# A two-layer trunk in split float32: value products without ScalarE's copy, the last group's scores of layer a later, and halves of a wide output block between the first blocks' ends

## The chip, the core and the metric

One core of a Trainium2 chip runs the whole program. TensorE (PE) multiplies and transposes, and loads its stationary operand ahead (PEld); VectorE (DVE) and ScalarE (ACT) do all element-wise work; SyncE (SP) issues the transfers, which 16 DMA engines carry. Each engine runs its instructions strictly in the order in which they were put on it, and waits at each for what that one needs. The metric is the device time of one execution, in microseconds (us).

## The reference

Two pre-norm residual layers on a 256 x 2048 float32 input, 16 heads of 128. Layer a is latent attention, layer b attends within blocks of 256 positions; as the sequence is 256 long, layer b is causal attention with a linear distance penalty (the distance table times a slope for each head). Cut to what matters:

```python
def mla_mixer(h, ...):                       # layer a
    proj = h @ w_in                          # query latent 512, kv latent 256, rotary key 64, gate 2048
    q  = (rms_norm(q_lat) @ w_q_up)          # 16 heads x (128 + 64 rotary)
    kv = (rms_norm(kv_lat) @ w_kv_up)        # 16 heads x (128 key + 128 value)
    ...                                      # norms of q and k, rotary part
    o = causal_block_attention(q, k, v, scale)   # softmax(q k^T) v for each head
    return from_heads(o) * silu(gate)
x = x + mla_mixer(rms_norm(x, norm_a), ...) @ w_out_a
x = x + moba_mixer(rms_norm(x, norm_b), ...) @ w_out_b
```

## The kernel before

**Split products.** Weights are float32. A tile of 1024 columns (512 KB) comes by DMA into `wr` (4 buffers); ACT makes its high part `wh` (line 147, 1.05 us), DVE the rest `wl` (line 151, 1.2 us), both in the fast float32r form, and a product is three float32r matmuls (high x high, high x low, low x high). So every weight tile passes SP's queue, ACT's queue and DVE's queue before PE can use it. `run` keeps four tiles loaded ahead. A `wr` buffer is free again when the `wl` of the tile four places earlier is done, and the next load, which stands in SP's queue, waits for that; whatever stands behind that load on SP waits as well.

**A head** (`head_steps`) has steps that the planner places apart:
- s1: scores on PE (`ps_s`), the mask added and the minimum taken on DVE (line 468), exponentials on ACT (470), their reciprocal and the scaling of the weights `sm` on DVE (475).
- s2: `sm` is turned by a DMA transpose that SP issues (446): first a copy into `pz` as two planes (layer a: on ACT, line 445; layer b: on DVE), then the transpose, then a copy back into `pz` on DVE (452).
- s2_parts: from `pz` ACT makes `ph` (494) and, for the 128 columns of the first query half, the float32 copy `p1` (497); DVE makes `pl` (495).
- s3: four value products (`ps_o`), then `og` (value times gate) on DVE (509), and `ohl`, the high part on ACT (510) and the low part on DVE (511). `ohl` is what the output projection reads.

**Layer a** treats its 16 heads in 8 groups of two. `turns` of a group (three steps with transposes `ps_ta`, a copy and the parts `sr` of query and key, lines 425 to 431) come ahead of its scores.

**The output of layer a** has eight blocks of 256 columns, o0 to o7. A block takes 16 steps, one for each head; step i needs the `ohl` of head i, and four steps share one weight tile. Blocks o0 to o3 run their steps 0 to 11 first, since heads 12 to 15 (groups 6 and 7) are late, then their steps 12 to 15; then o4 to o7, which are of the wide kind (`blk_both`: each step writes two accumulators of a bank each). I write o1.4 for step 4 of block o1.

**Reloads.** Behind the last group, SP loads x again into `xt` (line 806, four loads) and then the distance table over the causal mask in `c_sb` (line 802, 192 KB). The first reader of that table is `alibi` of layer b's first head on ACT (line 917), which belongs to that head's s1.

**The order** of all steps on PE is written by a planner, `ordered(main, side)`: `main` is a fixed list; `side` steps (turns, heads) are put in when the lags of what they need have run out. Lags are constants: `TU` is that from a group's turns to its scores. What ACT, DVE and SP get follows from the order in which the steps are written out and from a scheduler.

Of the kernel before, what the change touches and what calls it, by code (L numbers as in the profile page):

```python
# [20 lines left out]
F32 = mybir.dt.float32  # L21
# [7 lines left out]
P = 128  # L29
S = 256  # L30
# [15 lines left out]

PA, PB, LO, TU, TUB, S1, S2A, S2B, S3 = 9000, 6000, 6000, 3000, 10000, 4800, 6000, 9000, 3000
FLB = 4500
SLACK = 1.3
HOLD = 4500  # L50
PACE, PACEB = 600, 3500
# [26 lines left out]
def paired(v):  # L78

    return v.rearrange("p (g l e) -> p g e l", l=2, e=16)  # L80


def lines(v):

    return v.rearrange("p (g l e) -> p g l e", l=2, e=16)


def unpaired(v):

    return v.rearrange("p (g e l) -> p g l e", l=2, e=16)  # L90
# [3 lines left out]
def trunk(ctx: ExitStack, tc, xT, gains, cst, w_in_a, w_q_up, w_kv_up, w_out_a, w_in_b, w_out_b, outT):  # L94
    nc = tc.nc
# [3 lines left out]
    wk = pool("wk", bufs=2)  # L99
# [55 lines left out]
    class Step:  # L155
# [7 lines left out]
        def ready(self):  # L163
            if any(d.end is None for d in self.needs + self.after):
                return None
            return max([d.end + d.lag * SLACK for d in self.needs], default=0)

# [30 lines left out]
    def matmul(*args, **kw):  # L198
        chain(nc.tensor.matmul(*args, skip_group_check=True, **kw))  # L199
# [254 lines left out]
    def head_steps(h, scores, bias, vt, cost, needs, needs_v, after, lag, front, pace=PACE, away=0):  # L454

        st = {}

        def s1():  # L460
            ps = work("ps_s")
            scores(ps)
            b = bias()
            sm = wk.tile([P, 384], F32, tag="sm", name="sm", bufs=3)
            mn = wk.tile([P, 2], F32, tag="mn", name="mn", bufs=4)
            rs = wk.tile([P, 2], F32, tag="rs", name="rs", bufs=4)
            for t, sl in ((0, slice(0, 128)), (1, slice(128, 384))):
                nc.vector.tensor_tensor_reduce(sm[:, sl], ps[:, sl], b[:, sl], 1.0, 3.0e38, ALU.add, ALU.min,  # L468
                                               mn[:, t:t + 1])
                nc.scalar.activation(sm[:, sl], sm[:, sl], AF.Exp, bias=mn[:, t:t + 1], scale=-1.0,  # L470
                                     accum_out=rs[:, t:t + 1])
            ri = wk.tile([P, 2], F32, tag="ri", name="ri", bufs=4)
            nc.vector.reciprocal(ri, rs)
            for t, sl in ((0, slice(0, 128)), (1, slice(128, 384))):
                nc.vector.tensor_scalar(sm[:, sl], sm[:, sl], ri[:, t:t + 1], None, op0=ALU.mult)
            st["p"] = sm

        def s2():
            pz = st["z"] = wk.tile([P, 384], F32, tag="pz", name="pz", bufs=2)
            if away:  # L480
                fly(st["p"], pz, front)
            else:
                flip(st["p"], pz, front)
                s2_parts()

        def s2_back():
            tc.keep_in_program_order(nc.vector.tensor_copy(words(st["z"]), planes(st["p"])))  # L487
            s2_parts()

        def s2_parts():  # L490
            pz = st["z"]
            ph = wk.tile([P, S], F32R, tag="ph", name="ph", bufs=2)
            pl = wk.tile([P, S], F32R, tag="pl", name="pl", bufs=2)
            nc.scalar.copy(ph, pz[:, :S])  # L494
            nc.vector.tensor_tensor(pl, pz[:, :S], ph.bitcast(F32), op=ALU.subtract)
            p1 = wk.tile([P, P], F32, tag="p1", name="p1", bufs=2)
            nc.scalar.copy(p1, pz[:, S:])
            st["t"] = ph, pl, p1

        def s3():  # L500
            po = work("ps_o")
            ph, pl, p1 = st["t"]
            vh, vl, v1 = vt()
            matmul(po[:, :S], vh, paired(ph), start=True, stop=False)
            matmul(po[:, :S], vh, paired(pl), start=False, stop=False)
            matmul(po[:, :S], vl, paired(ph), start=False, stop=False)
            matmul(unpaired(po[:, P:S]), v1, lines(p1), start=False, stop=True)
            og = wk.tile([P, S], F32, tag="og", name="og")
            nc.vector.scalar_tensor_tensor(og, po[:, :S], 0.5, gate_of[h // 2][:, h % 2], op0=ALU.mult, op1=ALU.mult)  # L509
            nc.scalar.activation(lines(ogh[:, h]), unpaired(og), AF.Copy)  # L510
            nc.vector.tensor_tensor(lines(ogl[:, h]), unpaired(og), lines(ogh[:, h].bitcast(F32)), op=ALU.subtract)  # L511

        a = Step(s1, cost, S1, needs, bank=True, pace=pace)
        b = Step(s2, 0, away or lag, [a])
        if away:
            e = Step(s2_back, 0, lag - away, [b])
            side.append(e)
        else:
            e = b
        return a, b, Step(s3, 545, S3, [e] + needs_v, after, bank=True, pace=pace)  # L520

    main, side = [], []
# [165 lines left out]
    heads, turns_of = [], []  # L688


    def group_a(g):
        z = {}
# [41 lines left out]
        def turn(i):  # L734
            def f():
                if i == 0:
                    two, four = (2, P), (2, S)
                    qf, kf, rf = cut(shared(g % 2), two, two, (1, P))
                    qh, ql, kh, kl, rh, rl = cut(shared(g % 2, F32R), two, two, four, four, (1, P), (1, P))
                    z["q"], z["k"], z["r"] = (qf, qh, ql), (kf, kh, kl), (rf, rh, rl)  # L740
                ps = work("ps_ta")
                if i == 2:
                    for t in range(2):
                        transpose(ps[:, t * P:(t + 1) * P], z["rope"][:, t].rearrange("p h d -> p (h d)"), ident)
                    parts(ps[:, :S], 1.0, *z["r"], False)
                    return
                for h in range(2):
                    for t in range(2):
                        transpose(ps[:, h * S + t * P:h * S + (t + 1) * P],
                                            z["tok", t][:, 256 * i + P * h:256 * i + P * (h + 1)], ident)  # L750
                if i == 0:
                    parts(ps, gq_a, *z["q"], False)
                else:
                    parts(ps, col(G_KN), *z["k"], True)
            return f

        def scores(h):
            def f(ps):
# [4 lines left out]

        proj = blk_rows(w_q_up[:, 384 * g:384 * (g + 1)], lambda: lat_st["x"], q_done)
        proj += blk_rows(w_kv_up[:, 512 * g:512 * (g + 1)], lambda: [x[:, 4:] for x in lat_st["x"]], kv_done, PA)
        turns = [Step(turn(i), 440, TU, proj[-1:], sum((h[:1] for h in heads[2 * g - 4:2 * g - 2]), ()) if g > 1 else (), bank=True)
                 for i in range(3)]
        for h in range(2):
            heads.append(head_steps(2 * g + h, scores(h), lambda: c_sb[:, C_MASK:C_MASK + 384],
# [57 lines left out]
    outs_a = [(blk_cols if j < 4 else blk_both)(w_out_a[:, 256 * j:256 * (j + 1)], og, out_done_a(j), 4000) for j in range(8)]  # L827
# [20 lines left out]
            outs_a[2 * j][-1].needs.append(again)  # L848
    for b in outs_a[:4]:
        main += b[:12]  # L850
    for b in outs_a[:4]:
        main += b[12:]
    main += sum(outs_a[4:], [])


    x_b = x_a
# [184 lines left out]
```

## Time and profile before

| | |
|---|---|
| time, median of 3 executions | 750.37 us (749.97 to 752.09) |
| the profiled execution's own time | 748.94 us |
| its span, first to last instruction | 747.1 us |
| PE busy | 739.7 us (99%) |
| PEld, DVE, ACT busy | 689.6 (92%), 588.3 (79%), 490.2 us (66%) |
| granted TensorE clock | 1.0 in every slice |
| DMA | 153.13 MB, mean 205 GB/s |

A share of busy time is a mean over the whole program. A PE that is 99% busy can gain only what is left of the span; it can lose anywhere. Start and end of a PE instruction overlap its neighbours', so the time lost on PE is read from the distance between starts.

### The profile page before, as it was taken

Reading aid. Unit: us, or ns where it says so; the run is one execution under the profiler, and the core shown is the slowest. Engines: PE = TensorE matmul, PEld = TensorE weight load, DVE = VectorE, ACT = ScalarE, POOL = GpSimd, SP = SyncE. Lnnn points to the kernel's source line nnn. Section 1 sums busy time; section 2 is a strip of 40 time slices with the busy share of each in tenths; the row PEclk is TensorE's granted clock in tenths of the full one; section 3 lists DMA queues with packets and bytes.
Section 4 is the critical chain, followed back from the end, with each engine's and each line's share of the span. In section 5 each row is a group of like instructions: output and inputs, shape, how many; then the busy total and the mean of one; then the engine's idle time right before and its main releaser. Section 6 shows DMA issues by size and latency. Waiting matters only on the chain.

```text
span 747.1 us, 13205 instructions
## 1 busy us (share of the span) xinstructions
PE 739.7 (99%) x4766; PEld 689.6 (92%) x4766; DVE 588.3 (79%) x1247; ACT 490.2 (66%) x1043; POOL 0.2 (0%) x4
## 2 busy tenths in 40 slices
PE   9999999999999999999999999999999999999998
PEld 8999999999999999988889888898889988899997
DVE  6988899899998697765788877887778967878563
ACT  7867898888877565456667666675567766665441
POOL 0000000000000000000000000000000000000000
PEclk9999999999999999999999999999999999999999
DMA  8875765666657866666888768886778778767771
GB/s 293 277 208 156 198 172 166 183 157 177 167 179 204 278 218 200 203 198 204 226 226 206 209 184 234 237 207 194 212 223 224 197 212 226 225 202 204 239 223 51
DMA packets 148354, 153.13 MB, mean 205 GB/s; under 512 B 47296, under 2 KB 115520, under 8 KB 148288
## 3 DMA queue, kind: packets, MB, share of 16 engines
q1 hardware_dynamic: 148000, 152.14, 71.7%
q8 instruction: 37, 0.61, 0.3%
q14 instruction: 29, 0.24, 0.1%
q10 hardware_dynamic: 288, 0.15, 0.1%
HBM read 139.68 MB, written 2.10 MB: 190 GB/s over the span
## 4 chain that ended last, share of the span: by engine, by line
PE 92%; DVE 3%; DMA 3%; ACT 0%; issue 0%; SPq 0%; DVEq 0%; ACTq 0%
PE acc L199 85%; PE ps_s L199 4%; DVE wl L151 2%; PE ps_o L199 2%; DMA sm<-pz 1%; PE ps_ta L202 1%; DMA c_sb<-cst 1%; DMA wr<-w_in_a 1%; ACT wh L147 0%; DVE xt L410 0%; PE ps_lt L202 0%; DVE xhl L334 0%; DVE pz L487 0%; PE ps_r L199 0%; DVE og L509 0%
## 5 line engine op out<-in xcount | busy, mean ns | idle before, releaser
L147 ACT ACTIVATE wh<-wr 128x1024 fp32r<-128x1024 f32 (+3 forms) x265 | 288.2, 1091 | 142.4 <-PE acc L199 115.0
L151 DVE TENSOR_TENSOR wl<-wr,wh 128x1024 fp32r<-128x1024 f32 (+3 forms) x265 | 313.6, 1187 | 72.0 <-PE acc L199 39.8
L199 PE MATMUL acc<-wh,xhl 128*128 128x512 f32 (+1 forms) x896 | 260.0, 375 | 0.4 <-ACT wh L147 0.4
L199 PEld LDWEIGHTS acc<-wh,xhl 128*128 128x128 f32 x896 | 168.6, 190 | 21.1 <-ACT wh L147 0.7
L199 PE MATMUL acc<-xhl,wh 128*128 128x256 f32 (+1 forms) x768 | 173.3, 312 | 0.0
L199 PE MATMUL acc<-ohl,wh 128*128 128x256 f32 (+1 forms) x800 | 172.2, 306 | 0.1
L199 PE MATMUL acc<-wl,xhl 128*128 128x512 f32 (+1 forms) x448 | 162.3, 374 | 0.1
L199 PE MATMUL acc<-ohl,wl 128*128 128x256 f32 x512 | 140.4, 274 | 0.2 <-DVE wl L151 0.2
L199 PE MATMUL acc<-xhl,wl 128*128 128x256 f32 x512 | 140.2, 274 | 0.0
L199 PEld LDWEIGHTS acc<-ohl,wh 128*128 128x128 f32 x800 | 130.0, 191 | 6.2 <-DVE ohl L511 0.3
L199 PEld LDWEIGHTS acc<-xhl,wh 128*128 128x128 f32 x768 | 126.3, 191 | 6.6
L199 PEld LDWEIGHTS acc<-ohl,wl 128*128 128x128 f32 x512 | 98.3, 192 | 0.5 <-DVE wl L151 0.5
L199 PEld LDWEIGHTS acc<-xhl,wl 128*128 128x128 f32 x512 | 98.3, 192 | 0.2
L199 PEld LDWEIGHTS acc<-wl,xhl 128*128 128x128 f32 x448 | 84.5, 190 | 10.4 <-DVE wl L151 0.4
L199 PE MATMUL acc<-wh,xt 128*128 128x384 f32 (+1 forms) x192 | 57.4, 356 | 0.0
L470 ACT ACTIVATE sm<-sm,mn 128x128 f32<-128x128 f32 x64 | 29.1, 456 | 13.1 <-DVE mn L468 13.1
L199 PEld LDWEIGHTS acc<-wh,xt 128*128 128x128 f32 x192 | 35.0, 189 | 1.2
L199 PE MATMUL acc<-wl,xt 128*128 128x384 f32 (+1 forms) x96 | 33.6, 350 | 1.3 <-DVE wl L151 1.3
L494 ACT CAST ph<-pz 128x256 fp32r<-128x256 f32 x32 | 12.9, 404 | 18.5 <-DVE pz L487 10.8
L511 DVE TENSOR_TENSOR ohl<-og,ohl 128x256 fp32r<-128x256 f32 x32 | 13.5, 423 | 11.9 <-ACT ohl L510 11.4
L510 ACT ACTIVATE ohl<-og 128x256 fp32r<-128x256 f32 x32 | 13.9, 437 | 12.7 <-DVE og L509 12.7
L410 DVE TENSOR_TENSOR xt<-acc,xt 128x256 f32<-128x256 f32 (+1 forms) x36 | 15.4, 476 | 8.0 <-PE acc L199 8.0
(154 smaller groups left out, 723.1 us busy)
## 6 DMA issues: line engine op xcount, KB each, us to landing
wr<-w_in_b SPq DMA_DIRECT2D x128, 512.0 KB, 4.1
wr<-w_in_a SPq DMA_DIRECT2D x32, 512.0 KB, 4.1
wr<-w_out_a SPq DMA_DIRECT2D x32, 512.0 KB, 4.5
wr<-w_out_b SPq DMA_DIRECT2D x32, 512.0 KB, 4.3
wr<-w_in_a SPq DMA_DIRECT2D x15, 416.0 KB, 5.2
wr<-w_q_up SPq DMA_DIRECT2D x16, 384.0 KB, 3.8
wr<-w_kv_up SPq DMA_DIRECT2D x8, 512.0 KB, 3.9
xt<-xT SPq DMA_DIRECT2D x4, 512.0 KB, 5.3
```

Source lines behind the costliest of these rows:

```text
L147: nc.scalar.activation(self.ordering(self.h)[1], self.ordering(self.raw)[0], AF.Copy)
L151: nc.vector.tensor_tensor(self.ordering(self.l)[1], self.ordering(self.raw)[0], self.ordering(self.h.bitcast(F32))[1], op=ALU.subtract)
L199: chain(nc.tensor.matmul(*args, skip_group_check=True, **kw))
L202: chain(nc.tensor.transpose(*args))
L410: nc.vector.tensor_tensor(lines(y), unpaired(b[:, o:o + n]), lines(y), op=ALU.add)
L470: nc.scalar.activation(sm[:, sl], sm[:, sl], AF.Exp, bias=mn[:, t:t + 1], scale=-1.0, accum_out=rs[:, t:t + 1])
L494: nc.scalar.copy(ph, pz[:, :S])
L510: nc.scalar.activation(lines(ogh[:, h]), unpaired(og), AF.Copy)
L511: nc.vector.tensor_tensor(lines(ogl[:, h]), unpaired(og), lines(ogh[:, h].bitcast(F32)), op=ALU.subtract)
```

## The change

Three edits.
1. The copy `p1` goes; the float32 value product reads `pz` itself, stands first of the four, and the product with `pl` last. `pz` gets four buffers instead of two.
2. The lag from the turns of the last group of layer a to its scores is `TUL` = 4500 instead of `TU` = 3000.
3. The tail of the output of layer a: o4, a wide block, is cut in two halves of eight steps that stand between the ends of o1 and o2, and of o2 and o3.

```diff
+TUL = 4500
@@ s2
-            pz = st["z"] = wk.tile([P, 384], F32, tag="pz", name="pz", bufs=2)
+            pz = st["z"] = wk.tile([P, 384], F32, tag="pz", name="pz", bufs=4)
@@ s2_parts
-            p1 = wk.tile([P, P], F32, tag="p1", name="p1", bufs=2)
-            nc.scalar.copy(p1, pz[:, S:])
-            st["t"] = ph, pl, p1
+            st["t"] = ph, pl, pz[:, S:]
@@ s3
-            matmul(po[:, :S], vh, paired(ph), start=True, stop=False)
-            matmul(po[:, :S], vh, paired(pl), start=False, stop=False)
+            matmul(unpaired(po[:, P:S]), v1, lines(p1), start=True, stop=False)
+            matmul(po[:, :S], vh, paired(ph), start=False, stop=False)
             matmul(po[:, :S], vl, paired(ph), start=False, stop=False)
-            matmul(unpaired(po[:, P:S]), v1, lines(p1), start=False, stop=True)
+            matmul(po[:, :S], vh, paired(pl), start=False, stop=True)
@@ group_a
-        turns = [Step(turn(i), 440, TU, ...
+        turns = [Step(turn(i), 440, TU if g < 7 else TUL, ...
@@ trunk
     for b in outs_a[:4]:
         main += b[:12]
-    for b in outs_a[:4]:
-        main += b[12:]
-    main += sum(outs_a[4:], [])
+    o = outs_a
+    main += o[0][12:] + o[1][12:] + o[4][:8] + o[2][12:] + o[4][8:] + o[3][12:] + sum(o[5:], [])
```

Behind the turns of group 7, PE's order was o1.4 to 9, s1 of head 14, o1.10, s3 of head 12, o1.11, s1 of head 15, o2.0 to 2, s3 of head 13, o2.3 to 11, o3.0 to 4, s3 of head 14, o3.5 to 8, s3 of head 15, o3.9 to 11, o0.12 to 15, and so on. It is now o1.4 to 11, s3 of head 12, o2.0, s1 of head 14, o2.1, s3 of head 13, o2.2 to 4, s1 of head 15, o2.5 to 11, o3.0 to 8, s3 of head 14, o3.9 to 11, o0.12 and 13, s3 of head 15, o0.14 and 15, o1.12 to 15, o4.0 to 7, o2.12 to 15, o4.8 to 15, o3.12 to 15.

**Place 1: DVE, behind the turns of group 7.** `sm_3301` and `pz_3393` are of head 12, `sm_3327` of head 13; `sr1_3404` holds the parts of query and key of group 7. Before:

```order
L473 RECIPROCAL ri_3308<-rs_3303 128x2
L151 TENSOR_TENSOR wl_3348<-wr_3274,wh_3276 128x1024
L475 TENSOR_SCALAR sm_3301<-sm_3301,ri_3308 128x128
L475 TENSOR_SCALAR sm_3301<-sm_3301,ri_3308 128x256
L473 RECIPROCAL ri_3334<-rs_3329 128x2
L151 TENSOR_TENSOR wl_3378<-wr_3344,wh_3346 128x1024
L475 TENSOR_SCALAR sm_3327<-sm_3327,ri_3334 128x128
L475 TENSOR_SCALAR sm_3327<-sm_3327,ri_3334 128x256
L431 SCALAR_TENSOR_TENSOR sr1_3404<-ps_ta_3405,gq_a_119,sr1_3404 128x256
L151 TENSOR_TENSOR wl_3453<-wr_3374,wh_3376 128x1024
L452 COPY pz_3393<-sm_3301 128x2x384
L431 SCALAR_TENSOR_TENSOR sr1_3404<-ps_ta_3419,g_sb_70,sr1_3404 128x512
```

Now (`sm_3277` and `pz_3369` are of head 12, `sm_3303` of head 13, `sr1_3378` of group 7):

```order
L152 TENSOR_TENSOR wl_3324<-wr_3250,wh_3252 128x1024
L474 RECIPROCAL ri_3284<-rs_3279 128x2
L474 RECIPROCAL ri_3310<-rs_3305 128x2
L152 TENSOR_TENSOR wl_3354<-wr_3320,wh_3322 128x1024
L476 TENSOR_SCALAR sm_3277<-sm_3277,ri_3284 128x128
L476 TENSOR_SCALAR sm_3277<-sm_3277,ri_3284 128x256
L476 TENSOR_SCALAR sm_3303<-sm_3303,ri_3310 128x128
L476 TENSOR_SCALAR sm_3303<-sm_3303,ri_3310 128x256
L432 SCALAR_TENSOR_TENSOR sr1_3378<-ps_ta_3379,gq_a_119,sr1_3378 128x256
L152 TENSOR_TENSOR wl_3425<-wr_3350,wh_3352 128x1024
L432 SCALAR_TENSOR_TENSOR sr1_3378<-ps_ta_3393,g_sb_70,sr1_3378 128x512
L453 COPY pz_3369<-sm_3277 128x2x384
```

The key's `sr` (128x512) has moved ahead of head 12's copy back from the transpose; the scaling of head 12's weights has moved behind the second `wl`, and that of head 13 stands right behind it.

**Place 2: DVE, heads 14 and 15.** Before (`sm_3506` and `pz_3610` are of head 14, `sm_3547` and `pz_3650` of head 15; the scaling of `sm_3547` stands five rows above the first):

```order
L452 COPY pz_3610<-sm_3506 128x2x384
L495 TENSOR_TENSOR pl_3615<-pz_3610,ph_3614 128x256
L452 COPY pz_3650<-sm_3547 128x2x384
L151 TENSOR_TENSOR wl_3642<-wr_3598,wh_3600 128x1024
L495 TENSOR_TENSOR pl_3655<-pz_3650,ph_3654 128x256
L151 TENSOR_TENSOR wl_3684<-wr_3638,wh_3640 128x1024
L151 TENSOR_TENSOR wl_3715<-wr_3680,wh_3682 128x1024
```

Now (`sm_3512` and `pz_3612` are of head 14, `sm_3571` and `pz_3663` of head 15):

```order
L453 COPY pz_3612<-sm_3512 128x2x384
L474 RECIPROCAL ri_3578<-rs_3573 128x2
L476 TENSOR_SCALAR sm_3571<-sm_3571,ri_3578 128x128
L476 TENSOR_SCALAR sm_3571<-sm_3571,ri_3578 128x256
L496 TENSOR_TENSOR pl_3617<-pz_3612,ph_3616 128x256
L152 TENSOR_TENSOR wl_3604<-wr_3550,wh_3552 128x1024
L152 TENSOR_TENSOR wl_3642<-wr_3600,wh_3602 128x1024
L453 COPY pz_3663<-sm_3571 128x2x384
L496 TENSOR_TENSOR pl_3668<-pz_3663,ph_3667 128x256
L152 TENSOR_TENSOR wl_3681<-wr_3638,wh_3640 128x1024
L152 TENSOR_TENSOR wl_3713<-wr_3677,wh_3679 128x1024
```

Head 15's scaling, which its transpose needs, has moved behind head 14's copy back. On SP the load of `c_sb` stands right behind that of tile `wr_3836` (before: `wr_3829`), which goes into the buffer that the last row here, `wl_3713`, sets free (before: `wl_3715`, the last row there).

**Place 3: ACT, the last two heads' `ohl`, and PE around head 15's value products.** On ACT, `og_3728` is of head 14 and `og_3768` of head 15 before:

```order
L510 ACTIVATE ohl_74<-og_3728 128x256
L147 ACTIVATE wh_3753<-wr_3751 128x1024
L510 ACTIVATE ohl_74<-og_3768 128x256
L917 ACTIVATE alibi_5156<-c_sb_71 128x384
L147 ACTIVATE wh_3792<-wr_3790 128x1024
```

Now `og_3726` is of head 14 and `og_3772` of head 15:

```order
L509 ACTIVATE ohl_74<-og_3726 128x256
L148 ACTIVATE wh_3750<-wr_3748 128x1024
L915 ACTIVATE alibi_5124<-c_sb_71 128x384
L509 ACTIVATE ohl_74<-og_3772 128x256
L148 ACTIVATE wh_3798<-wr_3796 128x1024
```

`alibi`, which reads the distance table, has moved ahead of head 15's high part. On PE, before (`acc_3686` is block o3; behind the last row come o3.10 and 11, then o0.12 to 14, and only then o0.15, the first step that reads head 15):

```order
L199 MATMUL ps_o_3763<-ph_3654,vh_3192 128x256
L199 MATMUL ps_o_3763<-pl_3655,vh_3192 128x256
L199 MATMUL ps_o_3763<-ph_3654,vl_3193 128x256
L199 MATMUL ps_o_3763<-p1_3658,v1_3194 128x4x2x16
L199 MATMUL acc_3686<-ohl_74,wh_3640 128x256 x2
L199 MATMUL acc_3686<-ohl_74,wl_3684 128x256
```

Now (`acc_3225` is block o0; the rows of `acc_3225` below are the first of o0.14, and o0.15 follows it):

```order
L200 MATMUL ps_o_3767<-pz_3663,v1_3170 128x4x2x16
L200 MATMUL ps_o_3767<-ph_3667,vh_3168 128x256
L200 MATMUL ps_o_3767<-ph_3667,vl_3169 128x256
L200 MATMUL ps_o_3767<-pl_3668,vh_3168 128x256
L200 MATMUL acc_3225<-ohl_74,wh_3640 128x256 x2
L200 MATMUL acc_3225<-ohl_74,wl_3681 128x256
```

Between head 15's value products and the first step that reads their result stood six steps; now it is one.

## Rows read from the trace of the kernel before

**Rows 1.** The page, parts 1 and 2: busy time of each engine, and the granted clock in 40 slices of the span.

```profile
PE 739.7 (99%) x4766; PEld 689.6 (92%) x4766; DVE 588.3 (79%) x1247; ACT 490.2 (66%) x1043; POOL 0.2 (0%) x4
...
PEclk9999999999999999999999999999999999999999
```

**Rows 2.** The waits of PE's weight loads (PEld): who waits, for whom; us in total, times, longest.

```profile
PEld acc L199 <- DVE wl L151: 4.0, 8, 0.6
```

**Rows 3.** The chain that ended last, in order of time: start, us, what.

```profile
99.05 1.14 DVE wl L151
...
101.59 0.56 PE ps_o L199 x5
...
188.13 1.14 DVE wl L151
...
226.46 3.52 DMA sm<-pz
...
246.46 2.27 DVE wl L151 x2
249.19 8.01 DMA c_sb<-cst
```

**Rows 4.** PE's timeline at four places (a group before its value products, head 14's scores, the four block ends in a row, and the starts of o0.14 and o0.15): start, us, instruction, and what ended the idle time before it.

```profile
99.49 0.46 PE L199 MATMUL acc<-wh,xt 128*128 128x512 f32 x1
100.24 0.48 PE L199 MATMUL acc<-wl,xt 128*128 128x512 f32 x1 [0.29 <-DVE wl L151]
...
230.50 0.36 PE L199 MATMUL ps_s<-sr 128*128 128x256 f32 x1
231.29 0.50 PE L199 MATMUL ps_s<-sr 128*128 128x256 f32 x2 [0.42 <-DVE sr L431]
...
268.98 0.38 PE L199 MATMUL acc<-ohl,wh 128*128 128x512 f32 x1
269.59 0.38 PE L199 MATMUL acc<-ohl,wl 128*128 128x256 f32 x1 [0.23 <-DVE wl L151]
...
254.36 0.39 PE L199 MATMUL acc<-ohl,wh 128*128 128x256 f32 x2
...
255.03 0.39 PE L199 MATMUL acc<-ohl,wh 128*128 128x256 f32 x2
```

**Rows 5.** The copies into `p1` (`p` here) as one line of the program (duration in ns: least, median, most); then ACT's and DVE's timelines ahead of the wait at 99.05 of rows 3.

```profile
L497 ACT COPY p<-pz x32: 292/293/305, 93.4 to 680.6; 128x128 f32<-128x128 f32 x32
...
95.27 0.40 ACT L494 CAST ph<-pz 128x256 fp32r<-128x256 f32 x1 [0.50 <-DVE pz L452]
95.58 0.29 ACT L497 COPY p<-pz 128x128 f32<-128x128 f32 x1
95.78 0.47 ACT L425 ACTIVATE sf<-ps_ta,gq_a 128x256 f32<-128x256 f32 x1
...
97.38 0.69 ACT L430 ACTIVATE sr<-ps_ta,g_sb 128x512 fp32r<-128x512 f32 x1
...
98.10 0.75 DVE L431 SCALAR_TENSOR_TENSOR sr<-ps_ta,g_sb,sr 128x512 fp32r<-128x512 f32 x1
```

**Rows 6.** DVE's and ACT's timelines at head 12 and at the key's part `sr` of group 7.

```profile
225.03 0.54 DVE L475 TENSOR_SCALAR sm<-sm,ri 128x128 f32<-128x128 f32 x2
...
225.56 1.20 DVE L151 TENSOR_TENSOR wl<-wr,wh 128x1024 fp32r<-128x1024 f32 x1
...
230.00 0.60 DVE L452 COPY pz<-sm 128x768 uint16<-128x768 uint16 x1 [1.18 <-DMA sm<-pz]
230.50 0.73 DVE L431 SCALAR_TENSOR_TENSOR sr<-ps_ta,g_sb,sr 128x512 fp32r<-128x512 f32 x1
231.15 0.41 DVE L495 TENSOR_TENSOR pl<-pz,ph 128x256 fp32r<-128x256 f32 x1
...
225.60 0.83 ACT L445 COPY pz<-sm 128x768 uint16<-128x768 uint16 x1
```

**Rows 7.** SP's, DVE's and ACT's timelines at head 15 (transpose, copy back, `og`, high part, low part) and `alibi`.

```profile
241.10 1.23 SPq L446 DMA_TRANSPOSE sm<-pz  x1
...
244.42 0.60 DVE L452 COPY pz<-sm 128x768 uint16<-128x768 uint16 x1 [0.98 <-DMA sm<-pz]
...
251.21 0.42 DVE L509 SCALAR_TENSOR_TENSOR og<-ps_o,gate 128x256 f32<-128x256 f32 x1
...
253.24 0.41 ACT L510 ACTIVATE ohl<-og 128x256 fp32r<-128x256 f32 x1
...
253.69 0.42 DVE L511 TENSOR_TENSOR ohl<-og,ohl 128x256 fp32r<-128x256 f32 x1 [2.05 <-ACT ohl L510]
...
257.22 0.52 ACT L917 ACTIVATE alibi<-c_sb 128x384 f32<-128x384 f32 x1 [3.57 <-DMA c_sb<-cst]
```

**Rows 8.** Transfers, us from issue to landing: the transposes of 195 to 260 us (least, median, most), the loads of `w_out_a` of 205 to 262 us (the same), the load of `c_sb`; and a stretch of the windows view (us, busy time of PE, PEld, DVE, ACT, POOL, then granted clock, DMA share, GB/s).

```profile
DMA to landing us min/median/max: 2.8/3.4/4.3
...
DMA to landing us min/median/max: 3.4/4.6/7.9
...
c_sb<-cst SPq DMA_DIRECT2D x1, 192.0 KB, 8.0
...
246.00:258.00 12.00, 12.00 (x110) 12.00 (x109) 7.38 (x11) 4.29 (x7) 0.00 (x0) 1.00 1.07 344
```

More of the change, by code (lines that the diff above doesn't have):

```diff
@@ L765, in group_a @@
         proj += blk_rows(w_kv_up[:, 512 * g:512 * (g + 1)], lambda: [x[:, 4:] for x in lat_st["x"]], kv_done, PA)
-        turns = [Step(turn(i), 440, TU, proj[-1:], sum((h[:1] for h in heads[2 * g - 4:2 * g - 2]), ()) if g > 1 else (), bank=True)
+        turns = [Step(turn(i), 440, TU if g < 7 else TUL, proj[-1:], sum((h[:1] for h in heads[2 * g - 4:2 * g - 2]), ()) if g > 1 else (), bank=True)
                  for i in range(3)]
```

## The prediction, made before the changed kernel was run

> **What bounds the kernel now.** I read the page's busy times and clock first [rows 1]: PE is busy for 739.7 of 747.1 us, at full clock (2.4 GHz) in every slice. All stalls of PE together, start and tail included, are some 7 us, so no reordering can win more than a few, while a new wait on PE is paid in full. The next views say where PE stands still in the middle: the waits of its weight loads [rows 2], the chain [rows 3], then the timeline, where a stall is the distance between two starts less the usual one. Three kinds matter here [rows 4].
> - In five groups of layer a PE waits for `wl` just before the value products: 99.49 to 100.24 instead of some 0.2, so 0.5; the chain shows it from 99.05 to 188.13 [rows 3, 4]. With what is lost around it I count 0.6 each, 3.0 in all.
> - Once for `sr` at head 14's scores: 230.50 to 231.29, about 0.8. DVE's row tells why: head 12's copy back waited for its transpose until 230.00, and `sr` stood behind it [rows 6].
> - Once for `wl` at the four block ends in a row: 268.98 to 269.59, about 0.5.
>
> **Value products.** PE's four matmuls stay the same in number, form and size; a set takes 0.56 us [rows 3]. Order alone does not change that: 0. The `pl` product coming last lets PE begin before `pl` is there, where it waits for it at all.
>
> **p1 copies gone.** 32 copies of 0.29 us, after which ACT's next instruction starts 0.20 after it (95.58 to 95.78 [rows 5]). ACT idles between the two heads of a group (0.50 before 95.27), so only the second copy delays what follows: ACT's `sr` of the key ends at 98.07 (97.38 + 0.69), DVE's part starts at 98.10, and the `wl` of the 0.6 us stall is behind it. 0.20 earlier there is about 0.18 less on PE, five times: **-0.9**. Ends: 0 (DVE then waits for another input) and -3.0 (the stall goes whole). The nearest row is the 0.03 between ACT's end and DVE's start, so I take 0.9.
>
> **Scores of head 14 later, `sr` ahead of the copy back.** The stall at 230.50 goes: **-0.8**.
>
> **A new wait at head 12's value products.** Its softmax weights are now scaled behind the second `wl`: the scaling started at 225.03, just ahead of that `wl` (225.56, 1.20 long), and now starts some 1.2 later [rows 6]. ACT's copy, the transpose and the copy back follow in a row: the transpose issued at 226.46 and 3.5 long [rows 3] goes out at about 227.7; the copy back ends near 231.8, `ph` 0.5 later, `pl` at 232.8 (231.15 + 0.41 before, with the same 1.2). PE, which no longer has the scores of head 14 in between, gets there after eight output steps. A step takes 0.67 (254.36 to 255.03 [rows 4]); in before the scores of head 14 began near 230.4 (their second row is 230.50) and stood two steps earlier, so PE comes at 231.7 and is done 0.56 after that if nothing is missing. It ends at 232.9 or so instead of 232.3: **+0.8** with the handoff. Ends 0 (transpose in 2.8 [rows 8]) and 1.2.
>
> **Head 15: the term that decides.** In before, six output steps (4.0 us) lay between head 15's value products and the step that reads their `ohl`; the low part ended at 254.11 (253.69 + 0.42 [rows 7]), and o0.15 started at 255.03 [rows 4]. Now one step lies between, and on ACT `alibi` stands ahead of head 15's high part. `alibi` waited 3.57 us for `c_sb` in before [rows 7], where only `wh` tiles stood behind it, with time to spare. Now the last `ohl` stands behind it, and PE behind that. So when does `c_sb` land?
> Its load stands on SP behind a weight load which waits for a `wl`. In before that `wl` ended at 248.73 (246.46 + 2.27) and `c_sb` went out at 249.19 [rows 3]. Now the same place is two `wl` behind head 15's `pl`, and head 15 is later: its scaling stands behind head 14's copy back, which waits for head 14's transpose. Head 14's transpose goes out near 240.6 (scores at about 235, then DVE has a `wl`, `og` and the low part of head 12 to do first) and lands 3.4 later [rows 8], at 244.0; copy back 0.5, head 15's scaling 0.6, one `wh` and the plane copy on ACT (1.0 and 0.8): its transpose leaves at about 246.7, 5.6 later than in before (241.10 [rows 7]). In before 7.6 passed from there to the second `wl`; one `wl` of 1.2 is out of that stretch now, but `pl` waits 0.6 for `ph`: 7.1, so the `wl` ends at 253.8, 5.1 later than it did.
> The load ahead of the last-but-one `wl` goes out near 252.65 and lands 3.4 later at the least [rows 8], at 256.05. Behind it come a load of x, a weight tile (512 KB each) and `c_sb` (192 KB): at 344 GB/s [rows 8] 1.5, 1.5 and 0.55. `c_sb` lands at about 259.6, 5.3 after its issue; in before it took 8.0 [rows 3, 8], with more queued ahead. Then `alibi` 0.5, high part 0.41, low part 0.42 [rows 7]: 260.9. PE, with -0.8 and +0.8 from above, stands at o0.15 at 255.03 as before, and needs the low part 0.1 later: **+5.8**. Ends: 2.4 (both transposes in 2.8, `c_sb` in the shortest landing) and 8.6 (transposes 4.3, landing 4.6 [rows 8], partly one behind the other).
> On a transfer's length the Trainium skill, DMA: Bandwidth & Descriptors, section "Anatomy of one DMA — SWDGE (gpsimd) path", gives a fit of 2.0 us plus bytes over 436 GB/s, measured for another issuing path; by it, as an estimate, `c_sb` takes 2.45 us, which would cut this term to some 2.9. This case's trace does not agree: the same load took 8.0 us in a stretch with the DMA engines full (share 1.07 [rows 8]).
>
> **Block ends spread.** Halves of o4 stand between them, so additions and splits on DVE no longer come four in a row; the 0.5 at 268.98 goes: **-0.5** (ends 0 and -0.6). It is safer still if PE has just stood 5 us while DVE went ahead.
>
> **Four `pz` buffers** let layer b's copies and transposes go out earlier. PE has no stall in its middle that this could take: 0, give or take 0.4 at the last group.
>
> **Sum.** -0.9 - 0.8 + 0.8 + 5.8 - 0.5 = +4.4, made against the profiled execution, 748.94, so 753.3. That execution is 1.4 below the median of the runs shown (750.37); on the median it is **754.8**. The times of 749.97 to 752.09 say that about 0.3% (2.25 us) is what a measurement of this kernel tells from no change.
>
> **The rivals.**
> - *`c_sb` comes by its own shortest landing*, not behind the three loads: out at 254.3, landed 3.4 later, low part at 258.95: 3.8 instead of 5.8, so **752.8**. For it: the queue is empty before 252.65. Against: 8.0 in before, and it shares the engines with 1.5 MB issued within 2 us. By the page's fit it would be 751.9.
> - *Not slower: `c_sb` is there in time.* If its `wl` ends by 248.7, as in before, `alibi` is done when head 15's `og` comes; then only 0.42 + 0.41 + 0.42 for `og` and `ohl` plus handoffs, 1.4 in all, stand against the 0.67 of cover: +0.7 instead of +5.8, **749.7**. Each us that the `wl` ends later than 248.7 costs one. For it: my 253.8 is a chain of ten links, and a transpose can land in 2.8. Against: to win 5 us, head 15's transpose would have to leave as early as in before, and its scores on PE are 4 us later.
> - *The copies' 0.2 breaks the stall of five groups whole* (-3.0 instead of -0.9): **752.7**. Against: PE's wait is 0.6, ACT gives 0.2.
> - *Later still*: transposes at 4.3 and loads at 4.6 or more, each issued as the DMA engines are full: about 3 more, **757.8**.
>
> **How the numbers follow.** Forecast as summed 0.58; `c_sb` alone 0.12; in time 0.13; stall whole 0.07; later still 0.10. The likeliest's own range is 753.2 to 757 (the ends of head 15's transposes and of the first landing). The range takes in the middle rivals and half of the latest: 751.2 to 757.5. Faster by over 0.3% (below 748.1) needs `c_sb` in time and a part of the five stalls: 0.05. Within 0.3% (to 752.6): the rest of that case, half of the `c_sb` alone case, half of the stall case and the lower edge of the forecast: 0.21. Slower: 0.74.
>
> **What would show it.** In the changed profile's chain: `c_sb` (or `wl` ahead of it), `alibi`, high and low part of the last head of layer a, then o0.15 with 4 to 7 us of idle time on PE released by DVE's `ohl`. The five waits for `wl` at 99 to 188 us should be there still, shorter by about 0.2 each; the wait for `sr` at 230 and the one at 269 gone; a small one for `pz`, `ph` or `pl` near 232. I am wrong if PE's idle time before o0.15 is under 2 us, if the five waits are gone, or if a loss stands in layer b, where I see no change.

## The result

The changed kernel takes 760.96 us (median of 4 executions, 759.82 to 761.99), the kernel before 750.26 on the same chip: a ratio of 1.0137, interval 1.0113 to 1.0161. The forecast was 754.8, range 751.2 to 757.5: the sign and the place were right, the size was less than half of what came. The page, parts 1 and 2, of the profiled execution (761.99 us, span 760.2; it is the slowest of the four, so sizes read from it are at the upper end):

```profile
PE 744.1 (98%) x4766; PEld 692.6 (91%) x4766; DVE 587.8 (77%) x1247; ACT 484.4 (64%) x1011; POOL 0.2 (0%) x4
...
PEclk9999999999999889999999999999999999999999
```

Against [rows 1], PE is busy 4.4 us longer with the same number of instructions, and two slices of the clock are no longer full: something beside waiting happened. The waits of the weight loads, as in [rows 2]:

```profile
PEld acc L200 <- ACT ohl L509: 5.6, 1, 5.6
PEld acc L200 <- DVE wl L152: 4.7, 8, 2.1
```

The wait on ACT's `ohl` is new, and one of the eight on `wl` is 2.1 long (0.6 at most before). PE's timeline at four places: a group's value products, those of head 12, o0.12, and o0.15.

```profile
100.37 0.38 PE L200 MATMUL acc<-wh,xt 128*128 128x512 f32 x1
100.87 0.48 PE L200 MATMUL acc<-wl,xt 128*128 128x512 f32 x1
...
231.53 0.28 PE L200 MATMUL acc<-ohl,wl 128*128 128x256 f32 x1
233.05 0.46 PE L200 MATMUL ps_o<-pz,v 128*128 128x128 f32 x2 [1.25 <-DVE pz L453]
...
253.64 0.39 PE L200 MATMUL acc<-ohl,wh 128*128 128x256 f32 x2
255.93 0.38 PE L200 MATMUL acc<-ohl,wl 128*128 128x256 f32 x1 [1.90 <-DVE wl L152]
...
259.42 0.42 PE L200 MATMUL acc<-ohl,wl 128*128 128x256 f32 x1
265.11 1.04 PE L200 MATMUL acc<-ohl,wh 128*128 128x256 f32 x2 [5.27 <-ACT ohl L509]
```

Against [rows 4], the first pair is 0.50 apart instead of 0.75: the groups' wait is shorter. A part of this only moved: the float32 product holds up what follows it by 0.08, and it stood last of the four before and stands first now (where nothing waits, from the start of the four to the second product behind them it is 0.78 in both kernels). So the gain is better read from the start of the four products (first row before, second row now):

```profile
99.01 0.27 PE L199 MATMUL ps_o<-ph,vh 128*128 128x256 f32 x1
...
99.81 0.39 PE L200 MATMUL ps_o<-pz,v 128*128 128x128 f32 x2
```

From there to the product with `wl` it is 1.06 now instead of 1.23, 0.17 less.

Then come three losses: 1.4 at head 12, 2.1 at o0.12, 5.6 at o0.15. The instructions behind the last, in SP's, DVE's and ACT's timelines (as in [rows 7]):

```profile
243.84 1.11 SPq L805 DMA_DIRECT2D xt<-xT  x2
247.37 1.23 SPq L447 DMA_TRANSPOSE sm<-pz  x1
...
257.53 0.49 SPq L801 DMA_DIRECT2D c_sb<-cst  x1
...
253.23 0.61 DVE L453 COPY pz<-sm 128x768 uint16<-128x768 uint16 x1 [4.78 <-DMA sm<-pz]
...
254.65 2.35 DVE L152 TENSOR_TENSOR wl<-wr,wh 128x1024 fp32r<-128x1024 f32 x2
...
264.22 0.52 ACT L915 ACTIVATE alibi<-c_sb 128x384 f32<-128x384 f32 x1 [5.47 <-DMA c_sb<-cst]
264.65 0.41 ACT L509 ACTIVATE ohl<-og 128x256 fp32r<-128x256 f32 x1
...
265.09 0.43 DVE L510 TENSOR_TENSOR ohl<-og,ohl 128x256 fp32r<-128x256 f32 x1 [5.36 <-ACT ohl L509]
```

Head 15's transpose goes out at 247.37 and DVE waits 4.78 us for it, with two `wl` queued behind; the second ends at 257.00, and `c_sb` goes out at 257.53; `alibi` waits 5.47 for `c_sb`, with the last `ohl` behind. This is the chain that was forecast, 4.6 us later than forecast (`alibi` at 264.22 instead of 259.6). Transfers, issue to landing: that transpose, the two loads of x issued 3.5 and 3.0 us ahead of it, and `c_sb`.

```profile
sm<-pz SPq DMA_TRANSPOSE x1, 5.4
...
xt<-xT SPq DMA_DIRECT2D x1, 512.0 KB, 4.7
...
xt<-xT SPq DMA_DIRECT2D x1, 512.0 KB, 6.2
...
c_sb<-cst SPq DMA_DIRECT2D x1, 192.0 KB, 6.7
```

And the clock, in the windows view (us, busy time of PE, PEld, DVE, ACT, POOL, granted clock, DMA share, GB/s):

```profile
253.70:256.00 2.30, 0.40 (x4) 0.21 (x3) 1.83 (x4) 2.13 (x3) 0.00 (x0) 1.00 1.09 349
...
256.80:259.50 2.70, 2.70 (x16) 2.70 (x14) 2.21 (x5) 1.38 (x2) 0.00 (x0) 0.53 0.94 269
...
265.10:270.30 5.20, 5.19 (x23) 5.02 (x24) 3.36 (x6) 2.37 (x4) 0.00 (x0) 0.50 0.03 9
270.30:272.00 1.70, 1.70 (x14) 1.65 (x14) 0.49 (x1) 0.55 (x1) 0.00 (x0) 0.90 0.83 282
```

PE stood for most of 253.7 to 256, and from 256.8 it worked at half clock (1.2 GHz); it stood again to 265.1, and the clock came back near 270.3. That is 2.7 us at 0.53 and 5.2 at 0.50: 1.3 and 2.6, so 3.9 us of work time lost beside the waits themselves. The 1.3 lie ahead of the wait for `c_sb`, though: with the clock up PE would have stood there longer by about as much. So only the 2.6 behind that wait make the program longer, which e2 below bears out.

**A table by stretch.** The executions differ by up to 2 us in the first 10 us, where the first weight tiles arrive, and by up to 1 us more before the first scores (the changed kernel's execution waits there for `xt`, that of e2, with the same code, does not). That has nothing to do with the change. So I compare stretches between five marks on PE: the start of the first scores of layer a (`ps_s`), of the last transpose of group 7's turns (`ps_ta`), of layer b's sums of squares (`ps_st`), the end of layer b's last scores, and PE's end. Each number is a difference of two such times in the trace of one execution (us).

| kernel | scores to last turn | last turn to sums | layer b | its tail | granted clock |
|---|---|---|---|---|---|
| before | 144.59 | 85.17 | 351.07 | 81.01 | 1.000 |
| changed | 143.71 | 97.66 | 350.97 | 81.72 | 0.992 |
| e1 alibi late | 145.41 | 91.21 | 351.07 | 81.52 | 0.998 |
| e2 busy | 143.69 | 94.23 | 350.97 | 81.47 | 1.000 |
| e3 reload late | 143.76 | 89.94 | 350.97 | 81.79 | 1.000 |
| e4 without the lag | 143.84 | 85.85 | 351.06 | 81.54 | 1.000 |
| e5 the lag alone | 144.87 | 93.54 | 351.07 | 80.57 | 0.995 |
| e6 transpose alone | 145.33 | 89.55 | 351.07 | 81.65 | 0.999 |
| e7 value part alone | 143.73 | 86.67 | 350.95 | 81.46 | 1.000 |
| e8 last sr first | 143.72 | 84.07 | 351.07 | 81.62 | 0.999 |
| e9 c_sb first | 143.69 | 91.14 | 350.95 | 81.31 | 0.998 |
| e10 halves alone | 144.56 | 84.40 | 351.07 | 80.57 | 1.000 |
| e11 last sr first, tail | 143.68 | 85.18 | 350.97 | 80.57 | 1.000 |

The change wins 0.9 in the first stretch, loses 12.5 in the second and 0.7 in the tail; the rest of the 13.1 by which the spans differ is 0.8 ahead of the first scores. (The first stretch of e1 and e6 is 1.6 longer for one slow transpose at 181 us, of which more below.) A tail of 80.57 stands beside 81.01 with the same instructions (e5, e10, before), so 0.4 there is spread. In the second stretch e8 and e11, in which PE's order is the same up to there, differ by 1.1. A difference of about 1 us between two of these traces therefore counts only where the wait that makes it is named. Most of the 0.7 in the tail is such a wait, for a low part in layer b's last group (before, then changed):

```profile
681.32 0.90 PE L199 MATMUL acc<-ohl,wh 128*128 128x256 f32 x2
682.06 0.28 PE L199 MATMUL acc<-ohl,wl 128*128 128x256 f32 x1
...
693.81 0.38 PE L200 MATMUL acc<-ohl,wh 128*128 128x256 f32 x1
694.90 0.38 PE L200 MATMUL acc<-ohl,wh 128*128 128x256 f32 x1 [0.71 <-DVE ohl L510]
```

### The profile page after: what moved, and what is told of

It reads as the page before. It is cut to its first block, busy times and chain, and to the rows that moved or that the text cites. A ratio compares the mean times of both kernels' runs of the same rounds, so it can differ in the third digit from the quotient of the medians.

```text
span 760.2 us, 13165 instructions
## 1 busy us (share of the span) xinstructions
PE 744.1 (98%) x4766; PEld 692.6 (91%) x4766; DVE 587.8 (77%) x1247; ACT 484.4 (64%) x1011; POOL 0.2 (0%) x4
## 4 chain that ended last, share of the span: by engine, by line
PE 63%; DVE 1%; DMA 0%; issue 0%; ACT 0%; DVEq 0%; ACTq 0%
PE acc L200 61%; PE ps_s L200 1%; PE ps_o L200 1%; DMA sm<-pz 0%; DVE wl L152 0%; DVE pl L496 0%; DVE pz L488 0%; DVE sm L469 0%; DVE pz L446 0%; PE ps_r L200 0%; DVE sm L476 0%; DVE xt L958 0%; ACT ph L495 0%; DVE ohl L510 0%; DVE og L508 0%
## 5 line engine op out<-in xcount | busy, mean ns | idle before, releaser
L200 PE MATMUL acc<-ohl,wh 128*128 128x256 f32 (+1 forms) x800 | 175.1, 310 | 6.0 <-ACT ohl L509 5.3
L200 PEld LDWEIGHTS acc<-ohl,wh 128*128 128x128 f32 x800 | 132.6, 195 | 12.7 <-ACT ohl L509 5.6
```

## The experiments

The edits are shown cut to what matters, with names such as `transpose_of_head_15` for the instructions that the code keeps.

**Which edit.** e5 has the lag alone, e4 the two others without it.

```diff
+TUL = 4500                                        # e5: this and the line below are all
-        turns = [Step(turn(i), 440, TU, ...
+        turns = [Step(turn(i), 440, TU if g < 7 else TUL, ...
```

> The kernel before with TUL as its only change. Theory (the later scores of heads 14 and 15 make all the losses): the stretch from the last turn of group 7 to layer b's first sums of squares, 85.2 us in the kernel before and 97.7 in the changed one, is 96 to 98.5 here, and the time 1.2 to 1.6% above the kernel before. Rival, the loss needs the missing p1 copies or the halves of o4 as well (which shifted loads on SP): under 0.8%.

Measured: ratio 1.0105 (1.0082 to 1.0128), stretch 93.5. That is less than the range I gave, and above the rival's 0.8%: the lag alone makes most of the loss. Of the 4.1 us by which this stretch is shorter than in the changed kernel, 1.9 is the loss at head 12, which does not stand in e5's trace, and 1.3 the wait at o0.12, 0.8 here instead of 2.1. By these traces e5 loses 8.4 in that stretch and e4 0.7, so some 3.4 of the 12.5 come only with the lag and the other edits together. `alibi` stands ahead of head 15's high part, and the same wait at o0.15 stands in PE's timeline:

```profile
256.68 0.28 PE L200 MATMUL acc<-ohl,wl 128*128 128x256 f32 x1
262.23 0.58 PE L200 MATMUL acc<-ohl,wh 128*128 128x256 f32 x1 [5.28 <-ACT ohl L511]
```

> The changed kernel without TUL (value products and halves of o4 alone). Theory: all losses come by TUL, so the wait for c_sb, the wait for wl at o0.12 and the one at head 12's value products are gone, and -0.9 for the copies and -0.5 for the block ends are left, with 0.6 lost at layer b's last group: 749.5 (748.5 to 750.3). Rival, the four pz buffers or the spread block ends lose something of their own in layer a: above 752.

Measured: ratio 0.9995 (0.9982 to 1.0008), 750.61 against 751.29. The large losses are gone, as the theory said, but so is most of the gain: the stretch is 85.85, not the 84.7 that follows from the block ends, because the wait at head 14's scores is now longer:

```profile
230.63 0.48 PE L199 MATMUL ps_s<-xt,sr 128*128 128x256 f32 x2
232.44 0.39 PE L199 MATMUL ps_s<-xt,sr 128*128 128x256 f32 x1 [1.33 <-DVE sr L431]
```

In before the key's `sr` stood behind head 12's copy back; here the key's has moved ahead of it, and the last, small `sr` (128x128) has stayed behind it.

**Alibi's place, or its table?** e1 puts `alibi` behind head 15's high part on ACT; e9 leaves it ahead and loads `c_sb` before the reloads of x.

```diff
+                if h == 0:                        # e1, in bias(h)
+                    after(alibi, high_part_of_head_15)
```

> The changed kernel with one thing put back: layer b's first alibi stands behind head 15's high part on ACT, as in the kernel before. If alibi's wait for c_sb holds up the last ohl (theory), the 5.6 us on PE ahead of o0.15 shrink to the handoff of og, high and low part, under 1 us; the 2.1 us wait for wl at o0.12 stays; the clock still falls after that wait, but for a shorter stretch. Time: 761.0 - 5.3 - 1 to 2.5 for the clock = 753.5 to 755. Rival, another piece is as late (og or a weight tile behind it): the wait stays over 3 us under another name and the time above 757.

```diff
-    for j in range(5):                            # e9
+    for j in (4, 0, 1, 2, 3):
         again = Step(reload(j), 0, 4000, [again])
```

> The changed kernel with the load of c_sb ahead of the four reloads of x (ACT's alibi then stands even ahead of head 14's high part). Theory (alibi held up the last ohl only because its table came late): PE's wait ahead of o0.15 is under 1.5 us as in e1, though alibi stands ahead on ACT; but 192 KB more stand ahead of head 15's transpose, so the wait for wl at o0.12 is 2 to 2.6 and the clock may fall. Stretch from the last turn to layer b's sums of squares 91 to 94 (97.7 in the changed kernel, 91.2 in e1). Rival, alibi's place on ACT costs whatever c_sb does: 96 or more.

Measured: e1 1.0053 (1.0037 to 1.0069), 754.98, stretch 91.2; e9 1.0070 (1.0043 to 1.0096), stretch 91.1. Both take 6.5 us off the stretch. In e9's ACT timeline `alibi` waits for nothing:

```profile
247.13 0.53 ACT L915 ACTIVATE alibi<-c_sb 128x384 f32<-128x384 f32 x1
...
256.54 0.42 ACT L509 ACTIVATE ohl<-og 128x256 fp32r<-128x256 f32 x1 [0.68 <-DVE og L508]
```

In e1 the wait ahead of o0.15 is what the chain `og`, high part, low part leaves with one step of cover:

```profile
258.79 0.28 PE L200 MATMUL acc<-ohl,wl 128*128 128x256 f32 x1
260.17 0.38 PE L200 MATMUL acc<-ohl,wh 128*128 128x256 f32 x1 [1.10 <-ACT ohl L509]
```

So the loss at o0.15 needs both: `alibi` ahead of the last `ohl`, and its table late. Either undone, the 5.6 us become 1.3, a little over the 1 that I gave for e1. Of e1's 6.5, some 4.3 is this wait; a shorter wait for `wl` at o0.12 (1.5, where I had said that the 2.1 stays) and less time at half clock (3.5 us instead of 7.9) give the rest. In e9 the wait at o0.12 is 1.2, not the 2 to 2.6 that I gave.

**The clock.** e2 keeps PE at work where it would stand still; the results of the added products are not used.

```diff
+    main += [busy(30)] + o[0][12:15] + [busy(95)] + o[0][15:] + ...   # busy(n): n products of 128x128 ones into a free bank
-    main += o[0][12:] + ...
```

> The changed kernel with 125 small matmuls into an unused bank where PE stands still (30 ahead of o0.12, 95 ahead of o0.15); nothing else is moved. If PE's standing still brings the clock down (theory), the granted clock is 1.0 throughout and the stretch from 256 to 271 us loses no time at half clock: in the trace of the changed kernel 2.7 us at 0.53 and 5.3 us at 0.5 cost about 4.0, so 757 (756 to 758). Rival, the clock falls for another reason, or the halved stretch is hidden by a later wait: 760 to 762.

Measured: ratio 1.0101 (1.0076 to 1.0125), 758.91 against 751.29; stretch 94.23, 3.4 less than in the changed kernel. Of these, 1.0 lies ahead of o0.15, where the table landed earlier in e2's execution, and 2.4 behind it, where the changed kernel worked at half clock. By the ratios it is 2.7 us (1.0137 less 1.0101, of 750), but the two intervals overlap a little. PE's wait for `ohl` is as long, but full of work, and the clock stays:

```profile
260.00:265.00 5.00, 4.93 (x87) 4.76 (x84) 0.23 (x2) 0.85 (x2) 0.00 (x0) 1.00 0.90 305
265.00:271.00 6.00, 5.92 (x45) 5.54 (x46) 5.08 (x9) 4.61 (x8) 0.00 (x0) 1.00 0.28 88
```

So some 2.4 to 2.7 of the 10.7 us are the clock alone, and with the waits filled it does not fall. The clock was down at 256.8, before the longer wait began, so in this execution it fell behind the 2.1 us at o0.12 alone. Waits of this kind do not bring it down each time: in e1, with 1.5 at o0.12 and 1.3 at o0.15, it was 0.51 for 3.5 us behind them; in e3, with 1.6 and 1.3, it stayed up (first row e1, second e3). What decides that is open.

```profile
260.90:264.40 3.50, 3.50 (x19) 3.50 (x19) 1.82 (x2) 0.64 (x2) 0.00 (x0) 0.51 0.93 319
...
253.00:262.00 9.00, 5.98 (x44) 5.02 (x44) 7.10 (x11) 4.61 (x8) 0.00 (x0) 1.00 1.08 341
```

**Head 15's transpose.** e3 holds the reloads of x behind it, e6 the next weight tile too; both have `alibi` behind the high part, so they stand against e1.

```diff
-            nc.sync.dma_start(res["x"][...], xT[...])
+            i = nc.sync.dma_start(res["x"][...], xT[...])
+            after(i, transpose_of_head_15)         # e3; c_sb behind the last of them
+            if self.behind: after(i, transpose_of_head_15)   # e6, in W.load, for o4's first tile
```

> The changed kernel with the four reloads of x behind head 15's transpose on SP, and c_sb behind them; alibi then stands behind head 15's high part on ACT too, so this is to be held against e1. If the two loads of x ahead of it made head 15's transpose 5.4 us long instead of 3.4 (theory), it takes 3 to 3.6 now, the wait for wl at o0.12 falls from 2.1 to under 0.5, the clock stays at 1.0, and the time is 2.1 + 1 to 2.5 below e1: 749.5 to 752. Rival, the transpose is as long without them: no better than e1.

> As e3, and the weight tile that e3 left 0.5 us ahead of head 15's transpose is held behind it as well, so nothing is issued in the 3 us ahead of it. In e3 that transpose still took 5.4 us. Theory (a transpose waits for whatever large load was issued shortly before): it takes 2.7 to 3.2 us now, the wait for wl at o0.12 (1.6 in e3) is under 0.3, and the stretch from the last turn to layer b's sums of squares, 89.9 in e3, is 87.5 to 88.7. Rival, head 15's transpose is long for a cause of its own: 5 us again, stretch as in e3.

Measured: e3 1.0064 (1.0040 to 1.0087), e6 1.0072 (1.0048 to 1.0096): no better than e1, against the theory. The profiles say why only in part. In e3 a weight tile came to stand 0.47 us ahead of the transpose, which took 5.4 again. In e6 nothing was issued for 3.6 us, and it still took 4.3, with loads issued 1.3 us behind it. The wait for `wl` at o0.12 was 1.6 in e3 and 1.0 in e6, where I had given under 0.5 and under 0.3. The stretches of the two profiled executions (89.9, 89.6) are shorter than e1's, but the times are not: e1's profiled execution lost some 1.7 us of work at half clock, those of e3 and e6 none there, and both are the fastest of their four executions.

What the traces do show is a relation over all 208 transposes of layer a in the thirteen traces: how long the last 512 KB load (or smaller weight tile) issued earlier still has to run when the transpose is issued, against the transpose's own time to landing (worked out from the issue and landing of each).

| earlier load lands after the issue, us | transposes | least | median | most |
|---|---|---|---|---|
| up to 1, or none in flight | 81 | 2.72 | 2.76 | 4.49 |
| 1 to 2 | 41 | 2.72 | 3.07 | 3.38 |
| 2 to 3 | 49 | 2.96 | 3.41 | 4.84 |
| 3 to 4 | 30 | 3.78 | 4.46 | 5.52 |
| over 4 | 7 | 4.68 | 5.36 | 5.59 |

With over 2 us of a load left, a transpose lands 0.7 to 1.1 us after that load (medians of the rows); with next to nothing in flight it takes 2.76 in the median. Three of the first row took over 4.2: e6's head 15, and one at 181 us in e1 and in e6. What made those slow stays open. Head 15's transpose in the changed kernel fits the table in part: the second load of x had 3.2 left, for which the median is 4.46, and it took 5.4. In e1 and e2, with the same two loads ahead of it, it took 4.8. That the reloads of x made it long is not shown: the table is a relation and no experiment, and in e6, with nothing issued in the 3.6 us ahead of it, it still took 4.3.

**The two other edits, each alone.**

> The kernel before with the value products' part alone (no p1 copy, float32 product first, four pz buffers). Theory: the stretch from the first scores to the last turn of group 7, 144.6 us before, is 143.7, as in the changed kernel; layer b's last group loses 0.5, and the wait for sr at head 14's scores is as in e4 (1.5 instead of 0.8): ratio 0.9985 to 1.001. Rival, the gain of layer a is kept whole: 0.997 to 0.9985.

> The kernel before with the halves of o4 between the ends of o1, o2 and o3 as its only change. Theory: the wait at 269 us (0.5) goes and nothing else moves: the stretch from the last turn to layer b's sums of squares is 84.5 to 84.9 (85.17 before), ratio 0.9985 to 1.0005. Rival, the new order makes a wait of its own: 85.5 or more.

Measured: the value part alone (edit 1 of the diff) 1.0028 (1.0013 to 1.0043), slower than the kernel before and above the range that I gave; its stretches are -0.9, +1.5 and +0.45. Most of the 1.5 is the longer wait at head 14's scores (1.4 in its timeline) and two waits for `wl` of 0.4 at the block ends (one before). That is +1.1 in sum, or 1.0014; the measured 1.0028 has its lower end there. The rest does not stand in its profile, which is that of the fastest of its twelve executions. The halves of o4 alone (edit 3) measure 0.9993 (0.9979 to 1.0008): not to be told from no change, with the stretch 0.8 shorter as the waits at the block ends are gone and that for `sr` is 0.4 instead of 0.7.

**A version that beats both.** e8 is e4 with the steps s2 of heads 12 and 13 held until group 7's last turn has been written out, so that all three `sr` stand ahead of head 12's copy back, and with e1's edit.

```diff
+    heads[12][1].after += turns_of[7]
+    heads[13][1].after += turns_of[7]
```

> e4 (value products and halves, no TUL) with heads 12 and 13 turned after the last turn of group 7, so that head 12's copy back no longer stands ahead of the last sr on DVE, and alibi behind head 15's high part. Theory: the wait for sr (1.5 in e4) goes and no other over 0.4 comes, so the stretch from the last turn to layer b's sums of squares is 84 to 84.6 (85.85 in e4, 85.17 before), and the time 0.9965 to 0.9985 of the kernel before. Rival, head 12's value products wait instead: 85.5 or more, a ratio of 0.999 or more.

Measured: 0.9984 (0.9967 to 1.0001), 749.59, stretch 84.07. The interval reaches 1, so e8 by itself is not shown to be faster than the kernel before. The wait for `sr` is gone and nothing took its place:

```profile
230.07 0.69 PE L199 MATMUL ps_s<-sr 128*128 128x256 f32 x3
230.60 0.38 PE L199 MATMUL ps_s<-krf,sf 128*128 128x128 f32 x2
230.74 0.60 PE L199 MATMUL ps_s<-xt,sr 128*128 128x256 f32 x3
231.18 0.38 PE L199 MATMUL acc<-ohl,wh 128*128 128x256 f32 x2
```

e11 adds one thing: in layer b's last group a `wl` is held behind the last head's `pl` on DVE.

```diff
+            if "hold" in res:                     # in W.low
+                after(wl, res.pop("hold"))
+            if away and h == 15:                  # in s2_parts
+                res["hold"] = pl
```

> e8 with one wl of layer b's last group behind the pl of its last head on DVE. Theory: PE's wait for the low part there (0.95 in e8, 0.4 in the kernel before) falls to 0.5 or less, the stretch from the last scores of layer b to PE's end is 81.0 to 81.2 (81.62 in e8, 81.01 before), and the time 0.9965 to 0.9985 of the kernel before. Rival, the wl held back is missed by PE right after: no gain over e8.

Measured: 0.9971 (0.9958 to 0.9984), 749.08 against 750.71: faster than the kernel before. The tail is 80.57, 1.0 less than e8's and below the 81.0 to 81.2 that I gave; its waits of the weight loads hold no `ohl` any more, and the longest on `wl` is 0.4:

```profile
PEld acc L201 <- DVE wl L151: 2.8, 7, 0.4
...
PEld acc L201 <- ACT wh L147: 1.0, 1, 1.0
```

Its second stretch, though, is 85.18 and not e8's 84.07, with losses of 0.5 each at a head's value products (236.5) and for a `wl` (243.8) that e8's trace does not have, in the same order of instructions on PE. In these two traces the one difference takes up the other. So e11 is shown to be faster than the kernel before; that it is faster than e8 is not shown, as their intervals overlap.

## Why the prediction failed, step by step

- **Copies gone, -0.9**: right. The stretch from the first scores to the last turn fell from 144.59 to 143.71, 0.88; in e7 it is 0.86. From the start of the value products to the product with `wl`, each of the five groups takes 0.16 to 0.18 less; the wait became shorter and did not go, as the step said.
- **Scores of head 14, -0.8**: right for the changed kernel, in whose trace that wait does not stand. It hung on the lag: without it (e4, e7) the wait is longer than before, not gone.
- **New wait at head 12, +0.8**: right place and cause, too small. PE lost 1.4 for `pz` and some 0.5 more for `ph`, `pl` and the handoff, 1.9. The transpose took 4.6 instead of the 3.5 taken from before: a weight tile issued 1.3 us ahead of it landed 3.9 after its issue.
- **Head 15, +5.8**: the mechanism was right (the wait on ACT's `ohl`, `alibi` ahead of it, `c_sb` behind a `wl` that is late), and the term was mis-sized: 2.1 at o0.12, 5.6 at o0.15 and some 0.4 at the low part behind it, 8.1. The step that failed is "In before 7.6 passed from there to the second `wl`", which became the 7.1 of the forecast. It took over a transpose that DVE had 3.3 us after its issue (241.10 to 244.42 [rows 7]). In the changed kernel DVE's copy back started 5.9 after the issue (247.37 to 253.23; the transpose took 5.4 of it), so that stretch was 9.6. With an issue 0.7 later than forecast, the two `wl` ended at 257.0 (254.65 + 2.35) instead of 253.8. Two loads of x had come to stand ahead of that transpose on SP, and the forecast did not price it by them; how much of the 5.4 is theirs stays open, as said above. The first of the two `wl` was then late for o0.12, a wait that I had not seen at all; and `c_sb` took 6.7 instead of 5.3. That the wait at o0.15, 5.6, came out near the forecast 5.8 is luck: the table landed 4.6 later than forecast, and PE came to o0.15 some 4.5 later than forecast too, for the losses at head 12 and o0.12 and for the clock.
- **The clock**: the term that is missing. I read "full clock in every slice" and priced waits as waits. What it costs is 2.7 us by the ratios of e2, 2.4 by its trace behind o0.15, and 2.6 by the clock's rows there. As PE's time in the profiled execution, all 3.9 of the clock's rows count. With them and the mis-sized terms the sum is -0.9 - 0.8 + 1.9 + 8.1 + 3.9 - 0.5 + 0.7 (tail) = +12.4, against the +4.4 of the forecast; the three stretches give 12.3 (-0.9 + 12.5 + 0.7). The medians differ by 10.7, as the profiled execution is the slowest of its four.
- **Block ends, -0.5**: right; no wait at the block ends in the changed trace, and 0.8 less in e10, of which 0.3 is the shorter wait for `sr`.
- **Layer b's last group, 0 give or take 0.4**: wrong by a little, +0.7, and a loss in layer b is one of the signs of being wrong that the prediction names. On DVE a `wl` came to stand between the copies back and the last `pl`; e11, which holds it back, has the tail at 80.57, the shorter of the two values that the old order shows.
- **The fit for a transfer** of the Trainium skill, DMA: Bandwidth & Descriptors, section "Anatomy of one DMA — SWDGE (gpsimd) path" (by it, as an estimate, 2.45 us for `c_sb`): the trace stayed against it with 6.7. Where one weight tile went out just ahead of it, in e9, the same load took 3.6, the nearest to the fit that any of these runs shows.
- **The range**: its upper end, 757.5, held transposes of up to 4.3, not of 5.4, and no price for the clock. That the waits would be longer still had been given 0.10.

## What to carry to other kernels

Where a change puts a step close ahead of its reader, follow each engine's queue ahead of that step to the last item, also the one that belongs to a later stage: here a table for the next layer held up the last `ohl`, and its load stood behind everything else. Price a small transfer anew by what is in flight when it is issued, and do not take its length over from the old order: here the load of one table took 8.0, 6.7 and 3.6 us in three orders, and one head's transpose 3.3 and 5.4. And add to a wait of several us on TensorE what the clock can cost behind it: here about 2.6 us behind a wait of 5.6.

## What the runs showed of the hardware

- In the changed kernel the granted clock was 1.00 until 256.8 and 0.53 (near the level of 1.2 GHz) from there to 259.5, behind a wait of PE of 2.1 us that ended at 255.9; behind a wait of 5.6 it was 0.50 for 5.2 us, though PE was at work. With filler products in the same waits (e2) it stayed at 1.00. Behind waits of 1.5 and 1.3 us it was 0.51 for 3.5 us in one execution (e1), and behind 1.6 and 1.3 it stayed at 1.00 in another (e3).
- A transpose by DMA that takes 2.76 us (median of 81) with no large load, or under 1 us of one, left to run took 4.46 (median of 30) with 3 to 4 us of one left and 5.36 (median of 7) with over 4; three took 4.2 to 4.5 with next to nothing left.
